# Sixteen of 24 modulation column groups: summed over rows on GpSimd in place, then one product with a column of ones

## The chip, the core and the metric

The kernel runs on one core of a Trainium2 chip. The metric is the device time of one launch in microseconds. Five engines work side by side, each taking its own instructions in order: TensorE (PE; its weight loads are listed as PEld), VectorE (DVE), ScalarE (ACT), GpSimd (POOL) and SyncE (SP), which here only issues loads. Matmuls read SBUF and write PSUM. Engines wait for each other through semaphores.

## What is computed

The program is a two-block transformer on 512 latent tokens with 256 context tokens and width 1024. The part at issue is the modulation of the first block:

```python
def modulation(cvec, w, b):
    mod = jax.nn.silu(cvec) @ w + b
    return jnp.split(mod[:, None, :], N_MOD, axis=-1)

sh_a, sc_a, g_a, sh_f, sc_f, g_f = modulation(c, ada_w[l], ada_b[l])
csh_a, csc_a, cg_a, csh_f, csc_f, cg_f = modulation(c_ctx[None, :], ada_w[l], ada_b[l])
...
x = x + g_a * y_lat
x = x + g_f * expert_choice_ffn(modulate(x, norm2_g[l], sh_f, sc_f), ...)
```

`ada_w` has 1024 rows and 6144 columns. Of the context's modulation only the shift and the scale `csh_a`, `csc_a` are used. Beside it stands the gated linear recurrence over eight heads (`hgrn_direction`, both directions), which is the first of three token mixers.

## The kernel before

Weights arrive in tiles of 1024 rows by 256 columns (1 MB), row p + 128 kk on partition p, in a pool called `raw` with three buffers that all of these loads share; `wload` (L89) and `wload2` (L98, two halves of 128 columns) issue them on SP. A weight is then split into a high and a low part (`wsplit`, L105): ScalarE casts (L111), VectorE subtracts (L112). A projection (`lin_steps`, L120) is three matmuls for each of 8 row blocks.

The modulation is made in 24 groups of 256 columns by `mod_cols` (L226). Eight groups (0 to 7, the first shift and scale, for latent and context) are made before the recurrence. The other sixteen, 8 to 23, are needed later, and `hgrn` (L298) puts them behind its heads: `MODS` gives head 0 one group, heads 1, 3 and 5 two, heads 2, 4 and 6 one, and head 7 six. For a group, eight fp32 matmuls multiply a [128, 32] tile (`cst`: column 0 the latent vector, column 1 the context vector, the rest zero) with the row blocks, four side by side in the array (L234); ScalarE copies the four partial sums (L236), TensorE transposes them twice (L239), VectorE sums them (L241) and adds the bias (L242). `self.mod[:, j, q]` holds the result for latent (q = 0) and context (q = 1).

A head (`hgrn_head`, L314) projects queries, both gates and the output gate, forms the gates' products F, the keys Q and the queries R in 1536 and 1024 columns, and then goes through seven levels of block sizes. In a level ScalarE copies part of Q to `Xc` (L381), TensorE multiplies it with R into `lps` (L383), and VectorE multiplies R (L388) and Q (L389) by the block products, merges `lps` into AT under a mask (L390) and halves the block products `tot` (L393). The masks `lvm` come from `km`, loaded once on POOL's queue (L354) and converted on VectorE (L355). After the levels the states are updated (`ktp`, `ups`, L403 to L414) and read out (`ops`, L419 to L421).

A list scheduler orders the instructions of each engine when the program is built: projections of the next head stand between the levels of a head. The eight heads come in pairs that share the load of `v` (L303); the pattern repeats every 109.8 us. The merge of the first mixer follows (`merge`, L465).

Of the kernel before, what the change touches and what calls it, by code (L numbers as in the profile page):

```python
# [39 lines left out]
# columns of w_in  # L40
# [5 lines left out]
# columns of the parameter array of the first block  # L46
PC, PCC, PAB, PN1, PN2, PHG, PCV = 0, 8, 16, 64, 72, 80, 88
# columns of the parameter array of the second block
# [30 lines left out]
class Net:  # L79
# [9 lines left out]
    def wload(self, src, c0, n=256, k0=0):  # L89
        """[1024 rows from k0, n columns from c0] of a weight matrix, row p + 128 kk on partition p"""  # L90
        w = self.wp.tile([128, KK, 256], FT, name="raw", tag="raw", bufs=3)
        self.nc.sync.dma_start(w[:, :, :n], src.rearrange("(kk p) n -> p kk n", p=128)[:, k0:k0 + KK, c0:c0 + n])
        if self.ahead:
            a = self.ahead.pop(0)
            self.loaded[a] = self.eload(*a)
        return w
# [18 lines left out]
    def lin_f(self, *args, **kw):  # L115
        """ps[m, n] = W[:, c0:c0+m]^T X^T[:, t0:t0+n]"""
        for _ in self.lin_steps(*args, **kw):
            pass
# [11 lines left out]
    def lin_f2(self, w, x, halves=False):  # L130
        """two tiles of lin_f; in halves of the tokens when the second half of x comes late"""
# [7 lines left out]
    def lin_n(self, ps, w, c0, x, t0, n, start=True, stop=True):  # L139
        """ps[128 tokens, n] = X[t0:t0+128] W[:, c0:c0+n]"""  # L140
# [11 lines left out]
    def rstd(self, ss, n, dst):  # L152
        """dst = (ss / n + eps) ** -0.5"""
        nc = self.nc
        nc.scalar.activation(dst, ss, AF.Ln, bias=self.eps, scale=1.0 / n)
        nc.scalar.activation(dst, dst, AF.Exp, scale=-0.5)

    def log_sigmoid(self, dst, z, tmp):
        """dst = min(z, 0) - ln(1 + exp(-|z|)); tmp is overwritten"""
# [66 lines left out]
    def mod_cols(self, gs):  # L226
        """columns 256 g : 256 (g + 1) of the modulation, feature-major: four partial sums side by side, then their sum"""
# [18 lines left out]
    def pow_rstd(self, dst, ss, n, sub=None):  # L246
        """dst = (ss / n + eps) ** -0.5 for a few columns"""
# [4 lines left out]
    def norm_in(self):  # L252
        """self.hx: features by 512 latent tokens, self.hc: features by 256 context tokens, high and low parts"""
# [18 lines left out]
    def norm_in2(self, xn, ks):  # L272
        """features 128 k : 128 (k + 1) of the modulated tokens, for k in ks"""
        nc, sp = self.nc, self.ap
        one = self.ab
        # gain and shift per feature: latent (0, 1), context (2, 3)
# [21 lines left out]
    def hgrn(self):  # L298
        nc, sp, W = self.nc, self.ap, self.I["w_in"][0]
        for hd in range(8):  # L300
# [10 lines left out]
            self.mod_cols(range(MODS[hd], MODS[hd + 1]))  # L311
        self.dump("aT", self.aT)

    def hgrn_head(self, hd, v):  # L314
        """both directions of a head. Index d: 0 forward, 1 backward, tokens in natural order, 256 context then 512 latent.
        F: products of the forget gates over blocks; Q[:, d]: keys times the gates from the key to the end of its block;
        R[:, 1 - d]: queries times the gates from the start of their block to the query. With blocks of m tokens, the pairs
        in neighbouring blocks of m come from the forward keys of the even blocks with the forward queries of the odd ones,
        and from the backward keys of the odd blocks with the backward queries of the even ones: one product for both."""
# [29 lines left out]
        # forget gate sigmoid(z), key sigmoid(-z)  # L349
# [9 lines left out]
        # products inside a chunk, transposed: the diagonal, then one level per block size  # L359
# [9 lines left out]
        def zigzag(x, n, m):  # L369
            """[n / 2m blocks, 2 halves, m]: the first row of x in the even blocks of m, its second row in the odd ones"""  # L370
# [3 lines left out]
        for lv in range(7):  # L374
# [10 lines left out]
            # blocks of twice the size  # L385
# [9 lines left out]
        # states: chunks 0, 1 are the context, 2 to 5 the latents  # L395
# [26 lines left out]
        # read-out: norm over the head, silu gate  # L422
# [27 lines left out]
    def gates(self, gate):  # L450
        """sigmoid(h W_gate)^T, a few products at a time, between those of others; self.sig holds it"""
# [13 lines left out]
    def merge(self, gate, wproj, first):  # L465
        """y^T (+)= sigmoid(h W_gate)^T * (o W_proj)^T, o in self.br"""
# [73 lines left out]
    def rope_tables(self, w):  # L540
        """per token tile and feature of a head: gain times cosine, for its neighbour gain times signed sine;
        0: queries, times the scale of the scores, 1: keys"""
# [10 lines left out]
    def qk_stats(self, ps):  # L553
        """1 / rms of 2 token tiles of 4 heads of 64"""
# [8 lines left out]
    def qk_norm(self, dst, ps, stats, which, t):  # L563
        """dst[128, 2, 256] = 2 token tiles of 4 heads, normed, times the gain, rotated from tile t on"""
# [30 lines left out]
    def attn_keys(self, g):  # L595
        """[kh; kh] and [kl; kl] of a group of heads, 128 rows by 768 keys"""
# [16 lines left out]
    def attn_queries(self):  # L613
        """[qh; ql], 128 rows by 512 tokens for each head, where the read-outs of its group go later; in steps of 4 heads
        and 256 tokens: projection and statistics, norm and rotation, transposes, one step apart"""
# [32 lines left out]
    def attention(self):  # L648
        """groups of 4 heads, in pairs of heads, in tiles of 128 tokens: scores and exponentials of a step run with the
        transposes of the step before and the values of the one before that"""  # L650
# [21 lines left out]
    def turned(self, n):  # L672
        """room for a third of the turned exponentials of a pair of heads, partly where the latent features were"""
# [24 lines left out]
    def attn_turn(self, P, pt, t, a):  # L698
        """four of the twelve transposes of a step: keys 2 a, 2 a + 1 of both heads"""
# [20 lines left out]
    def attn_sums(self, k, sm):  # L720
        """one over the sums, for each feature of the heads"""
        nc = self.nc
        nc.vector.reciprocal(sm, sm)
        # the factors, split, and then what they scale in the places of the queries
# [6 lines left out]
    def attn_out(self, k):  # L731
        """over the sums, which go from columns of tokens to rows"""
# [13 lines left out]
    def row(self, dst, cols, j0):  # L746
        """dst[128, 1024] = the per-feature columns cols[:, j0:j0+8] as a row on every partition"""
# [8 lines left out]
    def out_proj(self):  # L756
        """x1 = x + g_a * (y W_out), its squares' sums and the router's products"""
# [37 lines left out]
    def route(self):  # L795
        """softmax over the experts of (x1 / rms * a2 + shift) W; the 64 tokens of each expert"""
# [15 lines left out]
        # the 64 largest of each expert, the lowest token first among equals  # L812
# [25 lines left out]
    def eload(self, src, e, k0):  # L838
        """rows 128 k0 : 128 (k0 + 2) of a matrix of expert e"""
# [16 lines left out]
    def pair_mm(self, src, p, lhs):  # L856
        """two tiles [64 e + slot, 512] = rows of expert 2 p + e times its matrix"""
# [68 lines left out]
    def norm_pair(self, x, pr, r, gain, dst, tmp, tag="b", bufs=3):  # L926
        """token tiles 2 pr, 2 pr + 1 of dst (high, low): (x r gain)^T, features by tokens"""
# [16 lines left out]
    def chunk_norm(self, t, g, tmp, gain, dst):  # L944
        """256 columns of a token tile of the residual are final: their squares; at the last ones the norm"""
# [13 lines left out]
    def mem_norm(self):  # L959
        """the normed memory tokens, features by tokens, in the place of the latent features"""  # L960
# [629 lines left out]
```

## Time and profile before

| | |
|---|---|
| median of 3 runs | 2608.99 us (2608.29 to 2609.91) |
| profiled execution, span from first to last instruction | 2604.0 us |
| TensorE busy | 2528.8 us, 97% |
| VectorE busy | 1214.8 us, 47% |
| ScalarE busy | 982.5 us, 38% |
| POOL busy | 91.7 us, 4% |

The profiled execution's own time is its span with what lies around it; the median of the runs lies 5.0 us above that span. Busy shares are means over stages that differ: in the recurrence VectorE is full while a head goes through its levels and idle for long pieces in between. TensorE's busy time contains the modelled tail of each matmul, so that the distance from one matmul's start to the next is the better price of one. Rows in the timeline merge neighbours of one kind: "x16" with 1.07 us is 16 records from the first start to the last end. An fp32 matmul leaves two records.

### The profile page before, as it was taken

The numbers are of one execution on the slowest core, as the hardware profiler recorded it, in microseconds if no ns is written. First come the engines' busy times: TensorE is split into PE (matmuls) and PEld (weight loads), VectorE is DVE, ScalarE is ACT, GpSimd is POOL, SyncE is SP. The second block draws the span as 40 slices with busy tenths as digits, with TensorE's granted clock in tenths as the row PEclk, the third lists the DMA queues.
The fourth block names the chain that finished last, engine by engine and source line by source line (L and its number), as shares of the span: only waits on it lengthen the run. The fifth ranks groups of instructions, "written<-read, shape, count | busy, mean of one in ns | idle before, by whom it ended". The sixth has DMA issues, their size and how long they took to land.

```text
span 2604.0 us, 35253 instructions
## 1 busy us (share of the span) xinstructions
PE 2528.8 (97%) x14796; PEld 1927.7 (74%) x14796; DVE 1214.8 (47%) x1934; ACT 982.5 (38%) x1649; POOL 91.7 (4%) x116
## 2 busy tenths in 40 slices
PE   6999999999999999999999999998998999999998
PEld 4888888689887976679744444444778988889898
DVE  4558575734443565544422222124884464532433
ACT  4445445532234466633301000003665443431332
POOL 0000000000001110120100000000000010000000
PEclk9999999999999999999999999999999999999999
DMA  8223222422223210054899999994330032223331
GB/s 272 65 81 98 81 66 65 146 97 81 89 90 97 81 65 1 1 193 157 305 409 409 407 363 363 361 361 136 81 97 17 22 109 65 90 81 98 97 98 49
DMA packets 242494, 380.60 MB, mean 146 GB/s; under 512 B 6672, under 2 KB 188944, under 8 KB 242336
## 3 DMA queue, kind: packets, MB, share of 16 engines
q1 hardware_dynamic: 238784, 365.98, 39.9%
q0 software_dynamic: 3552, 12.38, 1.5%
q8 instruction: 116, 1.90, 0.3%
q14 instruction: 42, 0.34, 0.0%
HBM read 372.04 MB, written 4.19 MB: 144 GB/s over the span
## 4 chain that ended last, share of the span: by engine, by line
PE 80%; issue 12%; DVE 3%; ACT 3%; DMA 1%; POOL 0%; SPq 0%; POOLq 0%; ACTq 0%; DVEq 0%
PE pair L864 15%; PE lin L125 10%; PE lin L126 10%; PE lin L127 10%; PE lin L145 6%; PE lin L147 5%; PE lin L146 5%; PE xtp L880 2%; PE oT L717 2%; PE sps L922 2%; PE lps L383 2%; PE s L690 2%; PE ptp L704 1%; PE ups L408 1%; PE lin L234 1%
## 5 line engine op out<-in xcount | busy, mean ns | idle before, releaser
L112 DVE TENSOR_TENSOR wl<-raw,wh 128x1024 fp32r<-128x1024 f32 (+1 forms) x262 | 312.2, 1227 | 213.8 <-ACT wh L111 210.7
L111 ACT CAST wh<-raw 128x1024 fp32r<-128x1024 f32 (+1 forms) x262 | 258.4, 1028 | 400.1 <-PE lin L126 249.5
L864 PE MATMUL pair<-ew,XT 128*64 128x512 f32 x1024 | 239.4, 595 | 0.0
L127 PE MATMUL lin<-hx,wl 128*128 128x512 f32 x576 | 231.4, 402 | 0.0
L125 PE MATMUL lin<-hx,wh 128*128 128x512 f32 x576 | 229.8, 399 | 0.0
L126 PE MATMUL lin<-hx,wh 128*128 128x512 f32 x576 | 227.9, 396 | 0.0
L864 PEld LDWEIGHTS pair<-ew,XT 128*64 128x64 f32 x1024 | 81.9, 136 | 145.8 <-issue 139.9
L145 PE MATMUL lin<-wh,mh 128*128 128x256 f32 x512 | 145.0, 283 | 0.0
L147 PE MATMUL lin<-wh,ml 128*128 128x256 f32 x512 | 144.7, 283 | 0.0
L146 PE MATMUL lin<-wl,mh 128*128 128x256 f32 x512 | 144.0, 281 | 0.0
L864 PE MATMUL pair<-ew,hT 128*64 128x512 f32 x512 | 142.7, 599 | 0.0
L125 PE MATMUL lin<-hxh,wh 128*128 128x512 f32 (+1 forms) x352 | 131.6, 376 | 1.4 <-ACT hxh L941 1.3
L126 PE MATMUL lin<-hxl,wh 128*128 128x512 f32 (+1 forms) x352 | 131.8, 375 | 0.1
L127 PE MATMUL lin<-hxh,wl 128*128 128x512 f32 (+1 forms) x352 | 131.4, 374 | 0.0
L127 PEld LDWEIGHTS lin<-hx,wl 128*128 128x128 f32 x576 | 108.3, 188 | 25.7 <-issue 1.0
L125 PEld LDWEIGHTS lin<-hx,wh 128*128 128x128 f32 x576 | 108.4, 188 | 24.6 <-issue 1.2
L126 PEld LDWEIGHTS lin<-hx,wh 128*128 128x128 f32 x576 | 108.3, 188 | 24.7 <-issue 0.2
L864 PEld LDWEIGHTS pair<-ew,hT 128*64 128x64 f32 x512 | 44.7, 136 | 73.1 <-issue 68.7
L146 PEld LDWEIGHTS lin<-wl,mh 128*128 128x128 f32 x512 | 96.8, 189 | 0.1
L145 PEld LDWEIGHTS lin<-wh,mh 128*128 128x128 f32 x512 | 96.6, 189 | 0.1
L147 PEld LDWEIGHTS lin<-wh,ml 128*128 128x128 f32 x512 | 96.3, 188 | 0.0
L915 DVE SCALAR_TENSOR_TENSOR ys<-pair,ws,gfrow 128x512 f32<-128x512 f32 x16 | 12.0, 750 | 173.2 <-PE pair L864 172.3
(539 smaller groups left out, 5586.1 us busy)
## 6 DMA issues: line engine op xcount, KB each, us to landing
ew<-in_w_gate SPq DMA_DIRECT2D x64, 1024.0 KB, 14.1
ew<-in_w_up SPq DMA_DIRECT2D x64, 1024.0 KB, 14.2
ew<-in_w_down SPq DMA_DIRECT2D x64, 1024.0 KB, 8.7
raw<-in_w_in SPq DMA_DIRECT2D x34, 1024.0 KB, 5.1
raw<-in_w_in SPq DMA_DIRECT2D x52, 512.0 KB, 5.4
raw<-in_ada_w SPq DMA_DIRECT2D x24, 1024.0 KB, 6.3
raw<-in_w_up SPq DMA_DIRECT2D x16, 1024.0 KB, 5.6
raw<-in_w_down SPq DMA_DIRECT2D x16, 1024.0 KB, 5.2
```

The lines of the kernel that those rows point to most:

```text
L111: nc.scalar.copy(wh[:, a:a + 4, :n], raw[:, a:a + 4, :n])
L112: nc.vector.tensor_sub(wl[:, a:a + 4, :n], raw[:, a:a + 4, :n], wh[:, a:a + 4, :n].bitcast(FT))
L125: self.nc.tensor.matmul(ps, a, xa, start=k == 0, stop=False)
L126: self.nc.tensor.matmul(ps, a, xb, start=False, stop=False)
L127: self.nc.tensor.matmul(ps, b, xa, start=False, stop=k == KK - 1)
L145: self.nc.tensor.matmul(ps, xa, a, start=start and k == 0, stop=False)
L146: self.nc.tensor.matmul(ps, xa, b, start=False, stop=False)
L147: self.nc.tensor.matmul(ps, xb, a, start=False, stop=stop and k == KK - 1)
L383: nc.tensor.matmul(ps[:, c].rearrange("p (b h x) -> p b h x", h=2, x=m), Xc[:, c], Y[:, c * n4:(c + 1) * n4], start=True, stop=True)
L690: nc.tensor.matmul(s[:, a:b], qT[2 * pair + hh][:, 128 * t:128 * t + 128], kT[p][:, a:b], start=p == 0, stop=p == 1)
L717: self.nc.tensor.matmul(self.oT[64 * hh:64 * hh + 64], self.vn[:, kt, 64 * g:64 * g + 64], PT[kt // 2][:, 2 * (kt % 2) + hh], start=kt == ...
L864: self.nc.tensor.matmul(ps[j][64 * e:64 * e + 64], lhs[:, k0 + k, 64 * e:64 * e + 64], w[e][:, k, 512 * j:512 * j + 512], start=k0 + k == ...
```

## The change

Groups 8 to 23 are made by a new function, `mod_sums`. POOL multiplies the loaded tile by the latent vector in place (one column per row block, broadcast over 256 columns: 2048 elements on each partition), and adds the eight row blocks in place in three steps (1024, 512, 256 elements). Two matmuls with the 128-column halves of the sum as stationary operand and a column of ones as moving operand add over the partitions, and VectorE adds the bias while reading PSUM. The context's column of these groups is no longer computed; nothing reads it. The first eight groups stay as they were. Comments and docstrings are removed too, which moves line numbers: lines from 256 on are 15 higher than before.

```diff
+    def mod_sums(self, gs):
+
+        nc, c = self.nc, self.cst
+        for g in gs:
+            w = self.wload(self.I["ada_w"][0], 256 * g)
+            nc.gpsimd.tensor_mul(w, w, c[:, :, 0:1].to_broadcast([128, KK, 256]))
+            for n in (4, 2, 1):
+                nc.gpsimd.tensor_add(w[:, :n], w[:, :n], w[:, n:2 * n])
+            acc = w[:, 0]
+            ps = self.lin()
+            for a in range(2):
+                nc.tensor.matmul(ps[:, a:a + 1], acc[:, 128 * a:128 * a + 128], self.one, start=True, stop=True)
+            j = slice(2 * g, 2 * g + 2)
+            nc.vector.tensor_add(self.mod[:, j, 0], ps[:, 0:2], self.pa[:, PAB + 2 * g:PAB + 2 * g + 2])
...
-            self.mod_cols(range(MODS[hd], MODS[hd + 1]))
+            self.mod_sums(range(MODS[hd], MODS[hd + 1]))
```

On POOL's queue, from the input norms (`ss`) to the first work after the recurrence (`nss`), there stood before only the load of the masks (the numbers are those of buffers; `pc` is a parameter array):

```order
L1410 DMA pc_74<-in_cols_c 128x101
L250 ISA
L250 TENSOR_TENSOR ss_148<-ss_148,mhalf_70 128x2 [waits DVE_49] x3
L354 DMA km_796<-in_km 128x896 [waits PE_49]
L250 TENSOR_TENSOR nss_4836<-nss_4836,mhalf_70 128x8 [waits DVE_49,Activation_49]
```

Now 64 instructions stand there; these are the first groups, `raw_969` behind head 0's weights and `raw_1333` and `raw_1343` of head 1:

```order
L265 TENSOR_TENSOR ss_148<-ss_148,mhalf_70 128x2 [waits DVE_49] x3
L250 TENSOR_TENSOR raw_969<-raw_969,cst_132 128x2048 [waits DMAHW3_49,DMAHW0_49,DMAHW6_49,DVE_49,PE_49]
L369 DMA km_796<-in_km 128x896 [waits PE_49]
L252 TENSOR_TENSOR raw_969<-raw_969 128x1024 [waits Pool_49]
L252 TENSOR_TENSOR raw_969<-raw_969 128x512 [waits Pool_49]
L252 TENSOR_TENSOR raw_969<-raw_969 128x256 [waits Pool_49]
L250 TENSOR_TENSOR raw_1333<-raw_1333,cst_132 128x2048 [waits DMAHW4_49,DMAHW5_49,DMAHW1_49,DMAHW7_49,DMAHW0_49,DVE_49]
L252 TENSOR_TENSOR raw_1333<-raw_1333 128x1024 [waits Pool_49]
L252 TENSOR_TENSOR raw_1333<-raw_1333 128x512 [waits Pool_49]
L250 TENSOR_TENSOR raw_1343<-raw_1343,cst_132 128x2048 [waits DMAHW1_49,PE_49]
L252 TENSOR_TENSOR raw_1333<-raw_1333 128x256 [waits Pool_49]
L252 TENSOR_TENSOR raw_1343<-raw_1343 128x1024 [waits Pool_49]
```

The mask load has moved behind a product that waits for its own load, each addition waits for the instruction before it, and the long product of a second group stands in front of the last addition of the first.

On TensorE, in head 7 behind the last level, the fourth group's four-way products stood in pieces between the head's own matmuls (`ups` updates, `ops` outputs; `ktp`, the second transposes of keys, comes next):

```order
L408 MATMUL ups_4031<-v_3210,kT_4021 128x128 [waits Activation_49]
L408 MATMUL ups_4031<-v_3210,kT_4021 128x128 x3
L408 MATMUL ups_4040<-v_3210,kT_4021 128x128 [waits Activation_49]
L234 MATMUL lin_4147<-raw_4145,cst_132 32x256 [waits DMAHW7_49,DVE_49]
L234 MATMUL lin_4147<-raw_4145,cst_132 32x256
L419 MATMUL ops_4065<-AT_3927,v_3210 128x128 [waits DVE_49]
L234 MATMUL lin_4147<-raw_4145,cst_132 32x256 x3
L420 MATMUL ops_4065<-R_3744,SA_4020 128x128 [waits DVE_49]
L234 MATMUL lin_4147<-raw_4145,cst_132 32x256 x3
L234 MATMUL lin_4164<-raw_4162,cst_132 32x256 [waits DMAHW0_49]
L234 MATMUL lin_4164<-raw_4162,cst_132 32x256 x2
L239 MATMUL lin_4147<-kc_61,mpart_4156 128x128 [waits Activation_49]
```

The last two groups are now read there, in one pair of products each (`raw_4054`, the fourth, just before the last level):

```order
L423 MATMUL ups_3961<-v_3147,kT_3951 128x128 [waits Activation_49]
L423 MATMUL ups_3961<-v_3147,kT_3951 128x128 x3
L423 MATMUL ups_3970<-v_3147,kT_3951 128x128 [waits Activation_49]
L256 MATMUL lin_4070<-ones_66,raw_4064 128x1 [waits Pool_49]
L256 MATMUL lin_4070<-ones_66,raw_4064 128x1
L434 MATMUL ops_3995<-AT_3857,v_3147 128x128 [waits DVE_49]
L256 MATMUL lin_4080<-ones_66,raw_4074 128x1 [waits Pool_49]
L256 MATMUL lin_4080<-ones_66,raw_4074 128x1
L435 MATMUL ops_3995<-R_3674,SA_3950 128x128 [waits DVE_49]
L418 MATMUL ktp_3974<-kc_61,Q_3672 128x128 [waits DVE_49]
```

Waits for POOL now stand between the updates and the outputs of head 7, the last of them in front of the second `ktp`. The loads of these three groups wait for the products of the three groups before them, which stand behind head 7's first level as they did before.

## Rows read from the trace of the kernel before

**Rows 1.** Busy by stretch: length, PE, PEld, DVE, ACT, POOL, granted clock, DMA, GB/s.

```profile
94.00:114.40 20.40, 20.00 (x135) 18.04 (x134) 20.02 (x32) 10.36 (x18) 0.00 (x0) 1.00 0.27 89
137.00:158.00 21.00, 20.65 (x173) 19.46 (x171) 20.61 (x34) 9.58 (x17) 0.00 (x0) 1.00 0.71 198
466.00:484.00 18.00, 15.22 (x128) 11.57 (x127) 17.14 (x31) 7.68 (x15) 0.00 (x0) 1.00 0.55 176
```

**Rows 2.** Timeline of a level of head 0: start, length, engine, line, operation.

```profile
101.20 0.94 DVE L389 TENSOR_TENSOR Q<-Q,tot 128x768 f32<-128x768 f32 x1
102.10 0.69 DVE L388 TENSOR_TENSOR R<-R,tot 128x512 f32<-128x512 f32 x1
102.22 0.62 ACT L381 COPY Xc<-Q 128x512 f32<-128x512 f32 x1 [0.67 <-DVE Q L389]
102.71 0.73 DVE L390 COPY_PREDICATED AT<-lvm,lps 128x512 f32<-128x512 uint8 x1
...
103.29 1.05 PE L383 MATMUL lps<-R,Xc 128*128 128x128 f32 x8
```

**Rows 3.** Timeline of TensorE: a group's products, and 128-column products in a run.

```profile
90.40 1.07 PE L234 MATMUL lin<-raw,cst 128*32 128x256 f32 x16
...
492.85 0.39 PE L421 MATMUL ops<-R,SA 128*128 128x128 f32 x2
493.07 0.39 PE L419 MATMUL ops<-AT,v 128*128 128x128 f32 x2
```

**Rows 4.** Groups of POOL's instructions: busy, mean ns, idle before and its releaser.

```profile
L500 POOL TENSOR_TENSOR yT<-yT,sig 128x512 f32<-128x512 f32 x16 | 21.6, 1351 | 149.6 <-DVE sig L499 149.5
...
L729 POOL TENSOR_TENSOR ao<-sm,ao 128x512 fp32r<-128x512 f32 x8 | 8.4, 1044 | 0.6
```

**Rows 5.** Timelines of POOL and DVE in the merges, two places.

```profile
776.20 2.70 POOL L500 TENSOR_TENSOR yT<-yT,sig 128x512 f32<-128x512 f32 x2 [61.30 <-DVE sig L499]
...
776.83 0.69 DVE L499 TENSOR_TENSOR sig<-lin,sig 128x512 f32<-128x512 f32 x1 [0.78 <-PE lin L127]
...
777.61 2.37 DVE L112 TENSOR_TENSOR wl<-raw,wh 128x1024 fp32r<-128x1024 f32 x1
...
1162.48 3.45 DVE L112 TENSOR_TENSOR wl<-raw,wh 128x1024 fp32r<-128x1024 f32 x2
1162.64 2.21 POOL L500 TENSOR_TENSOR yT<-yT,sig 128x512 f32<-128x512 f32 x1 [4.91 <-DVE sig L499]
```

**Rows 6.** Timeline of SP's loads, and the landing of the two from 88.63.

```profile
46.55 0.37 SPq L92 DMA_DIRECT2D raw<-in_ada_w  x1
...
88.63 3.27 SPq L92 DMA_DIRECT2D raw<-in_ada_w  x2
...
141.15 0.37 SPq L92 DMA_DIRECT2D raw<-in_ada_w  x1
...
418.08 5.47 SPq L92 DMA_DIRECT2D raw<-in_ada_w  x3
...
raw<-in_ada_w SPq DMA_DIRECT2D x2, 1024.0 KB, 5.4
```

**Rows 7.** Timelines of DVE and PE around head 0's weights and its chain.

```profile
63.43 2.36 DVE L112 TENSOR_TENSOR wl<-raw,wh 128x1024 fp32r<-128x1024 f32 x2 [9.40 <-ACT wh L111]
...
70.63 0.28 PE L125 MATMUL lin<-hch,wh 128*128 128x256 f32 x1
...
94.17 1.23 DVE L358 TENSOR_TENSOR R<-F,q 128x1024 f32<-128x1024 f32 x1 [0.46 <-ACT F L356]
```

**Rows 8.** Timeline of TensorE in head 7, its first level and its end.

```profile
467.10 1.49 PE L383 MATMUL lps<-R,Xc 128*128 128x128 f32 x8
...
495.00 0.48 PE L125 MATMUL lin<-hx,wh 128*128 128x512 f32 x1
```

**Rows 9.** Busy by stretch with the granted clock, in the attention.

```profile
942.20:945.00 2.80, 0.00 (x0) 0.00 (x0) 2.69 (x4) 2.68 (x7) 0.00 (x0) 1.00 0.94 324
946.10:952.90 6.80, 4.66 (x17) 3.79 (x16) 3.88 (x5) 4.70 (x10) 0.00 (x0) 0.50 0.30 100
```

## The prediction

> **What bounds the kernel now.** The change gives POOL work in one stage only, the recurrence over eight heads, about 44 to 495 us of the span, so I read that stage alone. The table of busy time by stretch comes first [rows 1]; POOL does nothing there yet. While a head runs its seven block levels (94.0 to 114.4 us for head 0, 137 to 158 us for head 1, and the same again every 109.8 us) TensorE is busy 20.00 of 20.40 us and VectorE 20.02 of 20.40: both are full, and at the full clock. Only in head 7, the last one, has TensorE gaps (15.22 of 18.00).
>
> The timeline of one level [rows 2] shows how they hang together. VectorE multiplies Q (101.20, two operands in SBUF), ScalarE copies the result to Xc (102.22 to 102.84), TensorE uses it at 103.29 (lps), and VectorE cannot multiply R (L388) before TensorE has read it. Between the levels TensorE runs projections of the next head, and their number is just enough: here 0.45 us lie between the copy's end and lps, and 0.5 between the end of the R before it and lps; the other levels look the same or tighter. TensorE takes its instructions in order. So **whatever stretches VectorE in a level chain stops TensorE almost one for one**, and nothing later gives it back, since TensorE is the full engine afterwards.
>
> **The change, part by part.**
>
> *Products saved.* A group loses 16 records of the four-way product (1.07 us) and two transposes, and gains two products with 128 stationary columns and one moving column. The pair of transposes is priced as two records in a run of 128-column products, where each two stand 0.22 us behind the two before; the new products, four records in fp32, as twice that, 0.44 us [rows 3]. So 1.07 + 0.22 - 0.44 = 0.85 us less on TensorE for each of the ten groups of heads 0 to 6: **-8.5 us**. The bounds are 0 (a lone product fetching new weights after a wait) and 16 x 0.85 = -13.6. The ScalarE copy and the reduction that go are off the path and are counted at nothing: ScalarE is busy 10.36 of 20.40 us there [rows 1], and a small addition takes the reduction's place.
>
> *POOL's work.* A group is one product over 2048 columns and additions over 1024, 512 and 256: 3840 columns in four instructions, each waiting for the one before. The nearest rows are POOL's two-operand instructions over 512 columns: 1.29 us each in the merge (two in 2.70 us with the gap between them [rows 5]; the mean of 1351 ns contains one that was held up) and 1.044 us in the attention [rows 4]. So a group takes 7.8 to 9.7 us of POOL.
>
> *What VectorE does meanwhile.* This carries the forecast. In the merge two POOL additions run from 776.20 to 778.90 us. A VectorE multiplication with one operand in PSUM runs beside them in its usual 0.69 us (776.83). But the subtraction L112, two operands in SBUF, begins at 777.61 and takes 2.37 us instead of 1.2: it ends 1.08 us after POOL does, so it stood still for 1.15 us of the second addition's 1.29. At 1162.48 two such subtractions take 3.45 us together, against 2.36 where POOL is idle [rows 5, 7], while POOL's addition, begun after the first of them, takes 2.21 instead of 1.29. The numbers fit one order only: subtraction, addition, subtraction. So the two engines exclude each other, and the waiting one goes next. 1.15 us per 512 columns is 8.6 us of hold per group (2048: 4.6, 1024: 2.3, 512: 1.15, 256: 0.57). The bounds are 6.8 (1.044 us less the 0.14 that did not hold) and 9.7 (the whole 1.29).
>
> The Trainium skill, "SBUF — State Buffer", section "Who interferes with whom", says the same of two SBUF inputs against a reading GpSimd, and that the first to issue has the shared pair for the whole instruction; the trace agrees at 512 columns (1.15 us of 1.29), and no row of it shows one of 2048. By that rule the long product holds VectorE for all of its time, as the sum below takes it; were it let go in pieces, the first rival would hold.
>
> *Where POOL's work falls.* The loads stay where they were. For an even head two groups are issued from 88.63 us and land 5.4 us later, from 94.0; for an odd head one is issued at 141.15; for head 6 three from 418.08 [rows 6]. POOL has nothing else to do and begins on landing, which is just when the chain begins: VectorE's first operation of it, L358, starts at 94.17 [rows 7]. From there nearly all of VectorE's instructions have two SBUF operands, so each of POOL's gets its turn behind one of them and delays the next. For an even head that is 2 x 8.6 = 17.2 us; for an odd head 8.6 less one masked copy (L390, one operand in PSUM, 0.73 us long, 0.6 without its overlap) that can run beside a hold [rows 2], 8.0. Heads 0 to 5: 3 x (17.2 + 8.0) = 75.6. Head 6, three groups with two such overlaps: 24.6. Minus 0.3 us of slack in each of seven chains: **+98 us**. By the bounds of the hold, 6.8 and 9.7 us a group, these twelve groups give 77 and 111.
>
> The very first group is issued at 46.55 [rows 6]. Its product, over by 46.55 + 5.4 + 5.2 = 57.2 us, now stands in front of the load of the masks (km) on POOL's queue, and their conversion on VectorE stands in front of a weight split. VectorE idles 9.40 us before that split, until 63.43; if the mask load too takes 5.4 us and some time to issue, conversion and split (2.36 us) end near 67, and TensorE's first product with the split weights starts at 70.63 [rows 7]. So I count nothing; without that cover it would be some 10 us.
>
> *Head 7.* Its last three groups can only be loaded when the first three have been read, right behind the first level (467.10 [rows 8]), about 467.7 us; 5.4 later, near 473.2, the first lands. From there POOL needs 25.8 us of holds and gives way to about ten VectorE operations of some 0.8 us: 507 us. The third product now stands in TensorE's order in front of the second transposes. So what is left by then is the product itself (0.44), five transposes (about 0.7), ten updates at 0.11 (1.1) and the outputs (492.85 to 495.00, 2.15), 4.4 us in all, which in the trace is done when the projections begin at 495.00 [rows 3, 8]: 507 + 4.4 - 495 = **+16 us**. If VectorE gives nothing away it is 473.2 + 3 x 7.8 or 9.7 = 496.6 or 502.3, so +6 to +12; at the upper hold +21. The merge's loads behind it hang on the first and second of these groups and come in time.
>
> *TensorE's clock.* In the trace it falls to half (0.50 granted, 1.2 GHz) after the engine has stood still for 2.80 us, and stays there 6.8 us [rows 9]. A hold of 4.6 us makes such a standstill, at least one in each chain. Inside a chain the slow clock costs less, since VectorE is late anyway. I take half of such a stretch, 3.4 us, to outlast the hold in each of the eight heads, and at half speed 1.7 us of it to be lost: **+14 us**; bounds 0 and the whole stretch, 8 x 3.4 = 27.
>
> *Sum.* 2604.0 (span) - 8.5 + 98 + 16 + 14 = 2723.5; the median of the runs lies 5.0 us over that span (2608.99): **2729 us**. All lower ends: 2604 - 13.6 + 77 + 6 + 0 + 5 = 2678; all upper ends: 2604 + 0 + 111 + 21 + 27 + 5 = 2768.
>
> **The rivals.**
>
> *Not slower: a long POOL instruction lets VectorE through.* For it: the rows show holds over 512 columns only, and a product over 2048 columns in eight blocks with a broadcast operand is another form. Against it: within 1.29 us there was no gap. Then the chains keep their pace, TensorE saves 8.5 us, and head 7 still waits 6 to 12 us for POOL: 2604 - 8.5 + 9 + 5 = 2609.5, 2605 to 2613. It decides from the point where the hold is under about 0.6 us a group.
>
> *VectorE keeps POOL out.* If back-to-back instructions of VectorE never let go, POOL's work slides behind each chain, into time when VectorE waits for TensorE (from about 114.4 us; two groups of 9.7 us end before their products are wanted near 135.6). Only head 7 pays: POOL starts at 484, ends at 513, +22 us: 2604 - 8.5 + 22 + 5 = 2622. Against it: the addition at 1162.64 did get in between two subtractions that stood back to back.
>
> *Half covered.* If the projections between the levels could be used up while VectorE stands (TensorE late at every second level only), half of the 98 and of the clock's 14 go: 2673. Against it: the order of TensorE's instructions is fixed, and the room is under half a microsecond.
>
> **How the numbers follow.** Forecast 0.76, not slower 0.08, POOL kept out 0.06, half covered 0.10. A measurement tells about 0.2% (5 us) from no change. Slower by more: the first, third and fourth, and a tenth of the rival that is not slower: 0.92. Within 0.2%: 0.06; faster: 0.02. The range takes in the forecast's bounds (2678 to 2768) and most of the half-covered case: 2655 to 2768, which leaves out 2605 to 2622 with 0.14 and some of the edges.
>
> **What would show it.** Right: VectorE's multiplications in the chains of heads 0 to 6 with maxima of 3 to 5.5 us instead of 0.95; POOL busy about 150 us more, its product near 4.7 us; TensorE idle some 12 to 17 us more in each even head and 8 in each odd one, waiting at lps; the granted clock at 0.50 in places before 490 us. Wrong: means of L388 and L389 unchanged beside a busy POOL (first rival); POOL's instructions long and late, ending behind the chains (second). If the stretch from 495 us on is longer, I have missed something behind the recurrence.

## The result, and the profile after

The changed kernel takes 2705.28 us (median of 4 runs, 2700.92 to 2706.11) against 2609.45 us (4 runs, 2608.29 to 2612.09): a ratio of 1.0367, 95% interval 1.0354 to 1.0381. That is 96 us more. The profiled execution took 2705.44 us with a span of 2703.7, 99.7 us longer than the span of before. The forecast was 2729, the range 2655 to 2768. So sign and range held, and the value was 24 us too high. In the rows that follow, lines of the kernel before from 246 on (not only from 256) stand 15 higher: its L358 is now L373, its L389 is L404.

Busy time by stretch, the same three places as in [rows 1] (columns as there): the level chain of head 0, of head 1, and of head 7.

```profile
95.50:116.30 20.80, 9.29 (x37) 7.44 (x36) 20.66 (x11) 5.58 (x9) 20.38 (x8) 0.77 0.26 82
154.00:175.50 21.50, 15.94 (x117) 15.48 (x117) 20.69 (x26) 8.54 (x13) 9.49 (x4) 0.92 0.47 133
543.40:578.00 34.60, 16.42 (x94) 15.20 (x94) 34.50 (x33) 9.18 (x15) 26.06 (x11) 0.65 0.38 122
```

VectorE is as full as before, but in head 0's 20.8 us it gets only 11 instructions done; in [rows 1] it got 32 done in 20.4. TensorE, which was busy throughout, works for 9.29 us, part of it at a lower clock. The timeline of POOL, VectorE and TensorE at the start of that chain shows why (`...` stands for rows left out, here projections on TensorE):

```profile
95.53 3.63 POOL L250 TENSOR_TENSOR raw<-raw,cst 128x2048 f32<-128x2048 f32 x1 [32.13 <-DMA raw<-in_ada_w]
95.57 4.67 DVE L373 TENSOR_TENSOR R<-F,q 128x1024 f32<-128x1024 f32 x1 [0.46 <-ACT F L371]
...
99.24 5.13 POOL L252 TENSOR_TENSOR raw<-raw 128x1024 f32<-128x1024 f32 x2
100.16 3.09 DVE L408 TENSOR_TENSOR tot<-F 128x768 f32<-128x768 f32 x1
103.18 1.75 DVE L377 TENSOR_TENSOR ks<-Q 128x512 f32<-128x512 f32 x1
104.33 4.06 POOL L250 TENSOR_TENSOR raw<-raw,cst 128x2048 f32<-128x2048 f32 x1
104.84 3.97 DVE L408 TENSOR_TENSOR tot<-tot 128x384 f32<-128x384 f32 x1
104.98 2.08 PE L380 MATMUL dps<-q,ks 128*128 128x128 f32 x8 [6.04 <-DVE ks L377]
106.84 1.91 PE L398 MATMUL lps<-R,Xc 128*128 128x128 f32 x8
...
115.89 0.55 PE L398 MATMUL lps<-R,Xc 128*128 128x128 f32 x1 [5.46 <-DVE R L403]
```

L373 was 1.23 us long [rows 7]. It now begins 0.04 us after POOL's product and ends 1.08 us after it: it stood for 3.44 of the product's 3.63 us. Each VectorE instruction behind it waits for one of POOL's in the same way, and TensorE waits 6.04 us for `ks` and 5.46 us for R. TensorE's longest waits from 40 to 600 us (sum, times, longest):

```profile
PE lps L398 <- DVE R L403: 60.3, 15, 9.6
PE dps L380 <- DVE ks L377: 19.8, 4, 6.0
```

Groups of instructions in the recurrence, POOL's and three of VectorE's:

```profile
L250 POOL TENSOR_TENSOR raw<-raw,cst 128x2048 f32<-128x2048 f32 x16 | 63.3, 3955 | 404.0 <-DMA raw<-in_ada_w 308.0 <-PE lin L147 95.9
L252 POOL TENSOR_TENSOR raw<-raw 128x1024 f32<-128x1024 f32 x16 | 47.3, 2953 | 0.7
L252 POOL TENSOR_TENSOR raw<-raw 128x512 f32<-128x512 f32 x16 | 26.2, 1639 | 1.3
L252 POOL TENSOR_TENSOR raw<-raw 128x256 f32<-128x256 f32 x16 | 19.8, 1235 | 0.7
...
L404 DVE TENSOR_TENSOR Q<-Q,tot 128x768 f32<-128x768 f32 x48 | 63.5, 1323 | 0.5
...
L403 DVE TENSOR_TENSOR R<-R,tot 128x512 f32<-128x512 f32 x48 | 49.1, 1023 | 10.1 <-PE lps L398 9.7
L405 DVE COPY_PREDICATED AT<-lvm,lps 128x512 f32<-128x512 uint8 x56 | 40.8, 729 | 0.0
```

The products of Q and R with two operands in SBUF, 0.94 and 0.69 us long in [rows 2], have means of 1.32 and 1.02; the masked copy, with one operand in PSUM, keeps its 0.73.

The granted clock fell too. Of thirteen stretches at 0.50 (1.2 GHz) between 46 and 590 us one stands here, with the sum of all (length, then PE and PEld busy):

```profile
103.44:110.27 6.83, 5.29 (x20) 4.58 (x20) 6.83 (x3) 0.59 (x1) 6.83 (x4) 0.50 0.00 0
...
sum 95.00, PE 58.48 PEld 54.83 DVE 88.55 ACT 21.77 POOL 75.24; mean PE 4.50 PEld 4.22 DVE 6.81 ACT 1.67 POOL 5.79
```

This one begins while TensorE stands and waits for `ks`. TensorE works for 58.5 us at half speed in all thirteen, so 29 us are lost there. One of the thirteen owes nothing to POOL: it runs from 45.4 to 48.83 us, before POOL's first product at 54.32, and makes 1.4 of the 29 us. Before, the clock stayed at 1.00 in the whole recurrence; the whole stretch (columns as in [rows 1]):

```profile
46.00:495.00 449.00, 442.95 (x2971) 379.22 (x2970) 285.13 (x446) 217.55 (x310) 0.00 (x0) 1.00 0.29 85
```

### The profile page after: what moved, and what is told of

Same layout as the page of the kernel before. It is cut to its first block, busy times and chain, and to the rows that moved or that the text cites. A ratio compares the mean times of both kernels' runs of the same rounds, so it can differ in the third digit from the quotient of the medians.

```text
span 2703.7 us, 34862 instructions
## 1 busy us (share of the span) xinstructions
PE 2546.3 (94%) x14572; PEld 1955.2 (72%) x14572; DVE 1310.1 (48%) x1918; ACT 977.3 (36%) x1633; POOL 247.5 (9%) x180
## 4 chain that ended last, share of the span: by engine, by line
PE 75%; issue 12%; DVE 7%; ACT 3%; POOL 1%; DMA 1%; SPq 0%; POOLq 0%; ACTq 0%; DVEq 0%
PE pair L879 14%; PE lin L125 9%; PE lin L127 9%; PE lin L126 9%; PE lin L145 5%; PE lin L146 5%; PE lin L147 5%; PE xtp L895 2%; PE oT L732 2%; PE sps L937 2%; PE lps L398 2%; PE s L705 2%; PE ptp L719 1%; DVE R L403 1%; DVE Q L404 1%
## 5 line engine op out<-in xcount | busy, mean ns | idle before, releaser
L398 PE MATMUL lps<-R,Xc 128*128 128x128 f32 x448 | 77.5, 326 | 62.3 <-DVE R L403 60.3
L398 PEld LDWEIGHTS lps<-R,Xc 128*128 128x128 f32 x448 | 69.3, 229 | 69.1 <-issue 63.8
L250 POOL TENSOR_TENSOR raw<-raw,cst 128x2048 f32<-128x2048 f32 x16 | 63.3, 3955 | 404.0 <-DMA raw<-in_ada_w 308.0
```

What stands on the lines that cost most here:

```text
L250: nc.gpsimd.tensor_mul(w, w, c[:, :, 0:1].to_broadcast([128, KK, 256]))
L398: nc.tensor.matmul(ps[:, c].rearrange("p (b h x) -> p b h x", h=2, x=m), Xc[:, c], Y[:, c * n4:(c + 1) * n4], start=True, stop=True)
```

## The experiments

The theory (A): POOL's reads of SBUF exclude VectorE's instructions with two SBUF operands, and since the level chains hang on VectorE, TensorE stops. Rivals: it is the changed order (B), any access of POOL (C), or only its two-operand form (D).

**Without the sums (e1), and with POOL's work beside the old products (e2).** e1 takes the four POOL instructions out and leaves everything else:

```diff
-            nc.gpsimd.tensor_mul(w, w, c[:, :, 0:1].to_broadcast([128, KK, 256]))
-            for n in (4, 2, 1):
-                nc.gpsimd.tensor_add(w[:, :n], w[:, :n], w[:, n:2 * n])
```

e2 keeps the old products for all groups (`mod_cols`) and puts POOL in front of those of groups 8 to 23 (`pool` is true for these):

```diff
             w = self.wload(self.I["ada_w"][0], 256 * g)
+            if pool:
+                nc.gpsimd.tensor_mul(w, w, self.ones[:, 0:KK, None].to_broadcast([128, KK, 256]))
+                for n in (6, 3, 2):
+                    nc.gpsimd.tensor_mul(w[:, :n], w[:, :n], self.ones[:, 0:n, None].to_broadcast([128, n, 256]))
```

> The changed kernel without POOL's four instructions: the two products read the loaded tile as it is, so that the sums over rows are left out; loads, products, additions of the bias and the order by the scheduler stay. Theory A (VectorE stands while POOL reads SBUF, and the level chains stop TensorE): no hold is left, only the saving on TensorE, 2609.5 minus 8.5 to 13.6, so 2596 to 2601 us; VectorE's L404 multiplication of Q back at a mean of 0.95 us. Rival B (not the hold but the changed order, with products that stand elsewhere and loads that come at other times, costs the time): most of the 96 us stay, over 2660 us.

> The kernel before with its four-way products, second transposes and reductions for all groups, and in front of each of the sixteen groups four POOL multiplications by ones in place (2048, 1536, 768 and 512 columns, made to last about as long as the change's four instructions, 8.5 us a group). Theory A: the whole loss and none of the saving, 2705.3 plus 8.5 to 13.6, so 2714 to 2719 us. Rival B (the new products and their order cost): near the kernel before, 2609 to 2630 us.

Measured: 2601.42 us without the sums (ratio 0.9973, 0.9964 to 0.9983, against 2608.69), and 2729.03 us with the old products and POOL's work (1.0461, 1.0446 to 1.0477). So POOL's work makes all of the loss, and B falls: the order of the new function without its sums is even 7 us faster. e2 lies 10 us above what was expected: POOL's four instructions there take 9.1 us a group where nothing meets them (the change's 8.1 to 8.4), and VectorE's busy time in the recurrence is 395.75 us against 285.13 in the kernel before, so 6.9 us of hold a group. Busy by stretch of the run without the sums and of the changed kernel, over the same part of the program:

```profile
46.00:488.80 442.80, 435.71 (x2762) 386.30 (x2763) 287.96 (x432) 213.92 (x297) 0.00 (x0) 0.98 0.31 93
```

```profile
46.00:589.40 543.40, 456.86 (x2763) 402.94 (x2762) 383.24 (x432) 213.64 (x295) 156.27 (x65) 0.91 0.25 74
```

The same 432 VectorE instructions take 95.3 us more with POOL beside them: 6.0 us of hold for a group on the mean of all 16. TensorE's idle time grows from 7.1 to 86.5 us.

**What in POOL's work holds VectorE.** Two runs put other instructions in the place of the four and leave the sums out; e3 has fills:

```diff
-            nc.gpsimd.tensor_mul(w, w, c[:, :, 0:1].to_broadcast([128, KK, 256]))
+            nc.gpsimd.memset(w, 0.0)
             for n in (4, 2, 1):
-                nc.gpsimd.tensor_add(w[:, :n], w[:, :n], w[:, n:2 * n])
+                nc.gpsimd.memset(w[:, :n], 0.0)
```

and e4 multiplications by a constant:

```diff
-            nc.gpsimd.tensor_mul(w, w, c[:, :, 0:1].to_broadcast([128, KK, 256]))
+            nc.gpsimd.tensor_scalar(w, w, 0.5, None, op0=OP.mult)
             for n in (4, 2, 1):
-                nc.gpsimd.tensor_add(w[:, :n], w[:, :n], w[:, n:2 * n])
+                nc.gpsimd.tensor_scalar(w[:, :n], w[:, :n], 0.5, None, op0=OP.mult)
```

> The changed kernel with POOL's four instructions replaced by fills of the same parts of the tile with zeros, which write and read nothing (the sums are left out). Theory A, that it is POOL's reading that excludes VectorE: VectorE's multiplications keep their old durations (L404 mean 0.95 us) beside a busy POOL, time as without the sums, plus up to 12 us if head 7 waits for POOL: 2596 to 2612 us. Rival C (any POOL access stops VectorE): VectorE stretched as long as POOL works; with fills of about half the length of the change's instructions about 2650 us, with the same length 2705 us.

> The changed kernel with POOL's four instructions replaced by multiplications by a constant in place over 2048, 1024, 512 and 256 columns: one operand read instead of two (the sums are left out). Theory A: VectorE stands for as long as each of them takes; the loss is in proportion to POOL's time for a group, 96 plus 10 us at 8.5 us a group and half of that at half: 2650 to 2705 us, with maxima of L404 as long as POOL's longest instruction plus 1 us. Rival D (only a POOL instruction with two operands stops VectorE): as with the fills, 2596 to 2612 us.

Measured: 2603.77 us with fills (e3; 0.9985, 0.9976 to 0.9994), 2678.02 us with one operand (e4; 1.0265, 1.0249 to 1.0281). The groups of the run with fills:

```profile
L250 POOL MEMSET raw<- 128x2048 f32 x16 | 29.0, 1814 | 401.0 <-DMA raw<-in_ada_w 319.4 <-PE lin L147 45.0 <-PE lps L398 36.6
...
L404 DVE TENSOR_TENSOR Q<-Q,tot 128x768 f32<-128x768 f32 x48 | 45.4, 946 | 0.9 <-ACT Xc L396 0.3
...
L164 DVE SCALAR_TENSOR_TENSOR F<-Q,F 128x1536 f32<-128x1536 f32 x8 | 14.1, 1759 | 79.7 <-ACT F L163 79.7
...
L408 DVE TENSOR_TENSOR tot<-F 128x768 f32<-128x768 f32 x8 | 7.6, 956 | 3.8 <-ACT F L371 3.8
```

POOL fills in the chains (95.12 to 102.4 us in head 0), and L404 keeps 0.946 us (0.945 in the run without the sums): these writes hold nothing, so C falls. One operand is enough to hold, so D falls too. The timeline of e4 at the start of head 0's chain:

```profile
94.02 1.23 DVE L373 TENSOR_TENSOR R<-F,q 128x1024 f32<-128x1024 f32 x1 [0.46 <-ACT F L371]
94.03 6.44 POOL L250 TENSOR_SCALAR raw<-raw 128x2048 f32<-128x2048 f32 x1 [28.82 <-DMA raw<-in_ada_w]
95.16 4.39 DVE L408 TENSOR_TENSOR tot<-F 128x768 f32<-128x768 f32 x1
```

Here VectorE came first by 0.01 us, and POOL's instruction, 5.4 us where it comes first, took 6.44. Then `tot`, 0.95 us alone, took 4.39: it stood for 3.44 us, as long as for the two-operand product, and ended 0.92 us before POOL did. So the one-operand form holds VectorE for 3.4 of its 5.4 us only; the expectation that VectorE stands for as long as POOL takes was wrong, and the loss is 69 us although POOL works longer (11.3 us a group on the mean against 9.8 in the changed kernel). Why it lets go early stays open. The Trainium skill, "SBUF — State Buffer", sections "Who interferes with whom" and "SBUF: two separate sides", says that a VectorE instruction with two SBUF inputs contends with a GpSimd instruction that reads, not with one that only writes, and that the first to issue blocks the other for the whole instruction. The runs agree on reading and writing and on the two-operand form (3.44 of 3.63 us); for the one-operand form they do not agree on the whole instruction.

**Which heads lose.** In e6 head 7's groups, three of which are loaded in head 6's chain, are made in the old way:

```diff
-            self.mod_sums(range(MODS[hd], MODS[hd + 1]))
+            (self.mod_sums if hd < 7 else self.mod_cols)(range(MODS[hd], MODS[hd + 1]))
```

In e8 only the single groups that fall into the chains of heads 1, 3 and 5 are new:

```diff
-            self.mod_sums(range(MODS[hd], MODS[hd + 1]))
+            (self.mod_sums if hd in (2, 4, 6) else self.mod_cols)(range(MODS[hd], MODS[hd + 1]))
```

> The changed kernel with head 7's six groups made in the old way; ten groups are still summed on POOL, in the level chains of heads 0 to 5. Theory A, each group costs where it stands: the trace of the changed kernel is 60.5 us late at the end of head 5 and 94.4 at the end of the recurrence, so 34 us go: 2669 to 2673 us. Rival F (the lateness is not additive, since a later wait takes it over): 2680 to 2705 us.

> The new function only for the groups of heads 2, 4 and 6: one group in each chain of heads 1, 3 and 5 and none in the others; all other groups in the old way. By the trace of the changed kernel an odd head is 3.9 to 4.4 us late, with two groups' saving of about 0.6 us each in it, so 5.2 us by its hold and clock: 3 times 5.2 minus 0.6, 14 us: 2621 to 2625 us. By the prediction, 8.0 us of hold and 1.7 of clock less 0.3 of slack and 0.85 of saving: plus 26, 2635 us.

Measured: 2671.77 us (e6; 1.0238, 1.0221 to 1.0255) and 2631.57 us (e8; 1.0088, 1.0073 to 1.0103), against 2608.86 in the same batch. The loss adds up by heads: 33.5 us go with head 7's groups, as expected, so F falls. The singles cost 22.7 us, not 14; the sum by the prediction's terms, 26, came nearer. An odd head's delay in the changed kernel (how much later the same VectorE and ScalarE instructions start than before) contains the saving on the pair that is read there and work moved between heads, so it was a poor measure; by the end of head 6 the three singles alone make 18.7 us of such delay, 6.2 each. The last 4 us come at the end of the recurrence. There the new programs, the changed kernel too, have some 24 records of the merge's projections done beforehand, and TensorE then waits 2.4 and 1.0 us for the cast and the split of head 7's output.

**Elsewhere, and in pieces.** If only the place costs, the sums should be free behind the chains. In e5 POOL's product reads a copy `cg` of the latent vector, which VectorE makes behind the levels (head 7 stays old); e9 takes `AT[:, 0, :KK]` in the place of `tot[:, :KK]`.

```diff
+        cg = sp.tile([128, KK, 1], FT, name="cg", bufs=2)
+        nc.vector.scalar_tensor_tensor(cg[:, :, 0], tot[:, :KK], 0.0, self.cst[:, :, 0], op0=OP.mult, op1=OP.add)
```

In e7 POOL's work of the changed kernel is cut into pieces of 256 columns:

```diff
-            nc.gpsimd.tensor_mul(w, w, c[:, :, 0:1].to_broadcast([128, KK, 256]))
+            for k in range(KK):
+                nc.gpsimd.tensor_mul(w[:, k], w[:, k], c[:, k, 0:1].to_broadcast([128, 256]))
             for n in (4, 2, 1):
-                nc.gpsimd.tensor_add(w[:, :n], w[:, :n], w[:, n:2 * n])
+                for k in range(n):
+                    nc.gpsimd.tensor_add(w[:, k], w[:, k], w[:, n + k])
```

> The changed kernel for heads 0 to 6, but POOL's product reads the latent vector from a copy that VectorE makes after the last level of the head whose chain the work had fallen into; so POOL starts behind that chain. Head 7's six groups are made in the old way. Ten groups are summed on POOL, as in the run with head 7's groups made in the old way. Theory A (the hold costs only where TensorE waits for VectorE): between the chains VectorE has room, nothing is lost, and the saving of ten groups is left: 2600 to 2608 us. Rival E (POOL's work costs wherever it stands, by holding VectorE's other work or by keeping tiles of the weight pool longer): 2620 to 2660 us.

> The changed kernel with POOL's work cut into pieces of 256 columns, eight products and seven additions a group: the same columns, the same results. Theory A with a clock that falls when TensorE stands for long: VectorE stands for the same sum but in short pieces; the standstill of 79 us against the kernel without the sums stays, the 21 us of slow TensorE shrink: 2685 to 2700 us. Rival G (short holds vanish in the slack between the levels): 2620 to 2660 us. Rival H (a fixed time for each POOL instruction adds to the hold): over 2710 us.

> As the late run, but the copy of the latent vector hangs on AT, which the last masked copy of the chain writes, and not on tot, whose last product runs early in a chain: in the late run the three single groups (151.84 us, 269.75 us) still fell into the chains of the odd heads. Theory A: the three singles cost 5 to 8 us each there and next to nothing behind the chain: 2642.3 minus 15 to 24, so 2618 to 2627 us. Rival E (POOL's work costs wherever it stands): 2636 to 2644 us.

Measured: 2642.31 us (e5; 1.0128, 1.0113 to 1.0143), 2658.66 (e7; 1.0194, 1.0178 to 1.0209) and 2634.17 (e9; 1.0101, 1.0086 to 1.0116; here the kernel before takes 2608.6, as for the three runs that follow). Against 2671.77 in the chains, the place is worth 29 and 38 us. But 26 us stay in e9: that nothing is lost between the chains was wrong, and E, though its range begins 2 us higher, is right there. Three more runs show what stays. In e12 only head 0's group and the three singles are new, the singles behind the chains; e10 is e9 in pieces, and e11 is e6 in pieces.

e12, against e9:

```diff
-            if hd < 7:
+            if hd in (0, 2, 4, 6):
```

> Only four groups on POOL: head 0's, under VectorE's idle stretch before 63 us, and the three singles behind the chains of heads 1, 3 and 5; all others in the old way. Theory A: no hold meets a chain, and four groups' saving of 0.9 us is left: 2603 to 2608 us, faster than the kernel before by 0.1 to 0.2%. Rival E: slower than before by 5 us or more.

> The same, with POOL's work cut into pieces of 256 columns. If pieces let VectorE's work between the chains through, the 3 to 4 us that each pair still costs an even head go as well: 2605 to 2616 us. If the loss of a pair there is POOL's lateness for the products, the longer work in pieces makes it worse: over 2625 us.

> Pieces of 256 columns in the level chains of heads 0 to 5, head 7's six groups in the old way: beside the run with whole instructions in the same place (2671.8 us). By the trace of the run in pieces, 17 us late at the end of head 5: 2623 to 2632 us. If the shorter work in pieces there was owed to head 7's groups, 2650 us or more.

Measured: 2630.34 us (e12; 1.0093, 1.0076 to 1.011), 2636.49 (e10; 1.0111, 1.0096 to 1.0126) and 2632.05 (e11; 1.0093, 1.0078 to 1.0108): e11 as expected, the other two in the upper of their two ranges. e12 is no faster than e8 (2631.57), which has the same three groups in the chains and head 0's group in the old way. The timeline of e12 behind head 1's chain:

```profile
156.16 3.60 POOL L250 TENSOR_TENSOR raw<-raw,cg 128x2048 f32<-128x2048 f32 x1 [93.89 <-DVE cg L416]
156.44 4.41 DVE L112 TENSOR_TENSOR wl<-raw,wh 128x1024 fp32r<-128x1024 f32 x1
160.76 0.34 DVE L437 SCALAR_TENSOR_TENSOR SA<-SA,tot,ups 128x128 f32<-128x128 f32 x1
161.16 0.49 PE L443 MATMUL ops<-R,SA 128*128 128x128 f32 x2 [2.87 <-DVE SA L437]
```

The state updates (L437) read PSUM and run beside POOL in their usual 0.35 us. But a weight split with two SBUF operands stands in front of them on VectorE and is held for 3.19 us, and TensorE's outputs wait 2.87 us for the update. The place behind the chain has a chain of its own. A pair behind an even chain (e9) costs 2 to 3 us a head: there the gates' difference F (L164), from which the next head starts, is held for 2.2 us (it is 1.76 us long alone):

```profile
124.51 3.93 DVE L164 SCALAR_TENSOR_TENSOR F<-Q,F 128x1536 f32<-128x1536 f32 x1 [2.19 <-ACT F L163]
```

In e10 the same instruction meets POOL's pieces:

```profile
123.51 10.27 DVE L164 SCALAR_TENSOR_TENSOR F<-Q,F 128x1536 f32<-128x1536 f32 x1 [2.19 <-ACT F L163]
123.95 4.05 POOL L251 TENSOR_TENSOR raw<-raw,cg 128x256 f32<-128x256 f32 x7
127.95 6.41 POOL L254 TENSOR_TENSOR raw<-raw 128x256 f32<-128x256 f32 x7
```

It takes 10.27 us instead of 1.76: fourteen of POOL's pieces follow one another without a gap, and F gets in only near 132.2 us, where POOL's last addition waits for the one before it. An even head costs 7 to 8 us there, while the single groups behind the odd chains, in pieces, make TensorE wait nowhere for more than 0.5 us. So e10 as a whole can't be told apart from e9 (the intervals overlap). In the chains the pieces do the opposite. In e7 a group of heads 0 to 5 takes POOL 13 to 18 us, a single VectorE multiplication in a chain is held by some 0.55 us at most, and VectorE's busy time is some 44 us above the run without the sums instead of 95. POOL's groups in head 0's chain, and TensorE's longest wait in head 7, which pays for it:

```profile
94.50 8.71 POOL L251 TENSOR_TENSOR raw<-raw,cst 128x256 f32<-128x256 f32 x8 [30.05 <-DMA raw<-in_ada_w]
103.18 8.84 POOL L254 TENSOR_TENSOR raw<-raw 128x256 f32<-128x256 f32 x7
```

```profile
PE lin L258 <- POOL raw L254: 18.2, 3, 7.9
```

What decides who stands is not shown. A gap in POOL's work is not needed: in e7's chain POOL's second piece starts at 95.07 us, before the first has ended, and VectorE's R still gets in between the two; in e9 F gets in behind one addition over 1024 columns though the next starts at 126.78 without a gap. The time of e7 lies in rival G's range (2620 to 2660), but the holds have halved and not vanished: not the number of columns that POOL reads sets the loss, but who has to stand. With whole instructions in the same place (e6 against e11) the loss is 63 against 23 us. In e7 and e11 an odd head, with one group in pieces and the saving on a pair, ends with 0.4 to 0.9 us less delay than the even head before it (by the copy of the head's output, `os`). A kernel with the singles alone in pieces wasn't run. It would lack the saving on the pairs, and the end of the recurrence costs every program that mixes the two functions about 4 us, so these numbers promise it no gain. No kernel that computes the whole beat the kernel before.

## Why the prediction was right, and where its sizes were off

By spans the forecast was 2723.5 - 2604.0 = +119.5, and the profile shows +99.7. Term by term:

| step | forecast | shown |
|---|---|---|
| products saved | -8.5 (0 to -13.6) | about -15 |
| holds in heads 0 to 6 | +98 (77 to 111) | TensorE idle +65 |
| head 7 | +16 (6 to 21) | TensorE idle +15 |
| TensorE's clock | +14 (0 to 27) | +29 |
| behind the recurrence | 0 | +5 |

TensorE's idle time is a stretch's length less its busy time, in the changed kernel for heads 0 to 6 11.5, 5.9, 11.4, 6.0, 12.4, 6.1 and 14.5 us; before it was 0.3 to 0.4 in each. The recurrence ends 94.4 us late. Less 65, 15 and 29 that leaves -15, which is the saving; the run without the sums gives the same -15 (6.2 us early, with 1.0 us more idle and 7.6 lost to the clock).

*Products.* The saving was counted for ten groups; for head 7's six nothing was counted, and TensorE had use for them: the saving lies beyond its bound of 13.6. It stays mixed with the work that the new order moves: the 24 records of the merge that now stand in this stretch take some 5.6 us (0.233 us each), so the saving itself is, as an estimate, rather larger than 15.

*The hold* was the right mechanism with a size too large. 8.6 us a group was a sum over four instructions, each scaled by columns from one addition over 512 [rows 5]. Two things were off. The product, with its small broadcast operand, takes 3.6 us for 2048 columns and not 4.7; the three additions take 2.4, 1.3 and 0.7 to 1.0 where nothing meets them, about as counted. So the group as a whole takes 8.1 to 8.4 us, in the lower part of 7.8 to 9.7. And VectorE does not stand for all of it: by head, the VectorE instructions are longer than the same forms without the sums by 13.7 us (head 0, two groups; forecast 17.2), 6.0 (odd heads; 8.0), 18.7 (head 6; 24.6) and 17.5 (head 7). About a quarter of POOL's time goes beside VectorE's work. The masked copies are a part of that, and the changes of turn may be another; the traces don't split it further. The twelve groups of heads 0 to 6 make 78 us of hold, 6.5 each, just at the lower bound of 77 (the mean of 6.0 over all sixteen contains the first group, which held next to nothing). The words "almost one for one" were right in the main: 78 us of hold, 65 us of idle TensorE, and some of the rest while TensorE ran at half speed.

*Head 7* came out right in size, for a partly different reason. POOL's last addition ends at 579.5 us, and TensorE waits only 0.4 us for it; 13 us are waits for R in the last levels, where VectorE is held for 17.5 us. Neither the chain nor POOL is much later than the other, so the good size is partly luck. (The prediction's upper end of 21 us works out to 20 by its own terms: 473.2 + 29.1 + 8 + 4.4 - 495.)

*The clock* was mis-sized by half. Half of one 6.8 us stretch in each of eight heads gave 27 us of slow time; the profile has 95, with TensorE busy in 58.5 of them, since a pair of groups makes more than one standstill (one pair keeps the clock down for 13.65 us), and head 7's triple keeps it down for 23.89. Even the upper bound of what is lost, 27, was too low, if barely. That the work at half speed is hidden behind VectorE's lateness is true only of a part.

*The first group* cost nothing, as forecast. The mask load moved behind the product, and its conversion now waits for it, but the split behind it still has 2.02 of the 9.40 us [rows 7] to spare; it starts 1.40 us late, and the copy of `v` long before it is late by the same 1.40, after a slow stretch of the clock from 45.4 us on:

```profile
61.44 1.36 DVE L370 CAST lvm<-km 128x896 uint8<-128x896 f32 x1 [8.07 <-DMA km<-in_km]
64.83 2.36 DVE L112 TENSOR_TENSOR wl<-raw,wh 128x1024 fp32r<-128x1024 f32 x2 [2.02 <-ACT wh L111]
```

*Behind the recurrence* some 4.5 of the 5.3 us come near 1800 us of the old span, where the clock is at 0.50 for 17 us instead of 6.8. The run without the sums loses as much there, so it is no effect of POOL. The 5.0 us taken as lying around the span were mostly such a difference between one execution and the median: in the changed kernel's own profiled execution 1.7 us lie around it.

The rivals: *a long instruction lets VectorE through* is refuted by the holds of 3.44 us. *VectorE keeps POOL out* did not happen with whole instructions, but in part it did with pieces (13 to 18 us a group on POOL). Against it the prediction said that the waiting engine goes next; e10, where one VectorE instruction waits for fourteen pieces, shows that this is no rule. *Half covered* (2673) was the nearest from below, but TensorE's idle time follows VectorE's hold in all heads (65 of 78 us in heads 0 to 6).

## What to carry to other kernels

Work moved to an idle POOL is not free where it reads SBUF while VectorE's instructions with two SBUF operands are on the path: price it as a stop of VectorE for about three quarters of the time that POOL takes undisturbed (here 95 us for 16 groups of 8.1 to 8.4), and add what TensorE's clock loses by the standstills, here a third as much again. Look at VectorE's queue in the very stretch where POOL's inputs land; an instruction that is off the path counts too when one on the path stands behind it. Cutting POOL's work into small pieces brought the loss in a full VectorE chain from 63 to 23 us (e6, e11), and gained nothing behind the chains (e9, e10), where one VectorE instruction had to let a whole run of pieces pass. Which of the two comes about has to be measured.

## What the runs showed of the hardware that was not expected

- A one-operand multiplication on POOL over 2048 columns lasts 5.4 us and holds VectorE for 3.4 of them; a two-operand product with a broadcast column lasts 3.6 and holds for 3.44; a fill lasts 1.8 and holds for nothing.
- Fourteen POOL pieces in a row kept one VectorE instruction out for 8.5 us, while in a chain of VectorE multiplications the same kind of pieces were themselves put off, 13 to 18 us a group where whole instructions take 8.1 to 8.4 undisturbed. What decides between the two is not shown.
